# Expert activations turned by VectorE in 32x32 blocks, down weights read in whole rows, combine in a split one-pass format, final norm reordered

## The chip, the core and the metric

One core of one Trainium2 chip runs the whole program. The metric is the device time of one execution, in microseconds, as the median of several runs. All numbers are float32.

## What is computed

A decoder trunk of two layers on 256 tokens of 1024 features. Layer 0 (a state-space mixer, stick-breaking attention and a dense feed-forward block) and the attention of layer 1 are not touched by the change. What it touches is the routed feed-forward block of layer 1 and the last norm:

```python
def moe_swiglu(h, w_router, w_gate, w_up, w_down):
    logits = (h @ w_router).astype(F32)
    top_val, top_idx = lax.top_k(logits, TOP_K)
    gates = jax.nn.softmax(top_val, axis=-1)
    combine = jnp.sum(jax.nn.one_hot(top_idx, N_EXPERTS, dtype=F32) * gates[..., None], axis=-2)
    out = jnp.zeros_like(h)
    for e in range(N_EXPERTS):
        y_e = swiglu(h, w_gate[e], w_up[e], w_down[e])
        out = out + combine[..., e:e + 1].astype(h.dtype) * y_e
    return out
...
x = x + moe_swiglu(...)
return rmsnorm(x, final_norm)
```

There are 8 experts, 2 for each token. w_gate and w_up of an expert are 1024 x 3584, w_down is 3584 x 1024.

## The kernel before

The expert stage begins when the router has placed each token in a slot of each expert (at most 96 slots, in 3 groups of 32; a loop at the end of the program, `rest`, is for experts with more, and is skipped otherwise). The loop at L1485 goes over the experts. Each expert's hidden width of 3584 is worked in two halves h of 1792 (`HALF`), and a half lies in four quarters of 448 (`CW`) on four bands of 32 partitions: partition 32j + s holds slot s of a group, and quarter j of its columns. So one group's half is a tile of 128 x 448.

For each half, `side` (L1352) multiplies the gathered tokens `he` with the gate weights, in eight steps k over the 1024 inputs. A step takes one weight tile of 128 x 1792 from the ring, and for each group g and quarter j issues a matmul of 32 columns of weights (the tokens) against 448 moving columns; the four quarters use four column bands of the array. Each matmul in full float32 is two instructions in the trace. The result is in three PSUM banks `gu`, one for each group. `fn(..., AF.Silu)` on ScalarE writes `A`; a second `side` does the up weights; and VectorE multiplies bank and `A` back into `A` (L1514). The `gu` banks come in turn from a pool of four (`pg`).

The down projection contracts over the hidden width, so that width must be turned onto the partitions. `turn` (L1365) does so with TensorE transposes of 128 x 128 through a PSUM bank `mt` and a copy by ScalarE or VectorE into `aT`. For the first three of the seven 128-column blocks it is called after steps k = 2, 3 and 4 of the second half's gate; for the other four blocks after the third, fourth and fifth tile of the down stage. `down` (L1377) takes 14 weight tiles: `down_rows` (L227) reads, for a block i, 128 rows of two quarters j, each row 4 KB; the block that lies across both halves is two transfers of 64 partitions. The result is in two `yb` banks, and copied to `y`.

`back` (L1338) makes `selT`, the matrix of zeros and ones that puts slots back to tokens. `combine` (L1400) multiplies it with `y`, one token block t of 128 at a time, with four row bands of 32 partitions into four banks `cb`; VectorE adds each bank, times the router's weight, to `yacc`. The combine of expert e stands after steps k = 1 and 3 of the first gate half of expert e + 1; the last expert's stands in the final norm, from L1526.

The order of TensorE's instructions here is that of the program text (`InOrder`). The other engines' order is set by the framework's scheduler. Weight tiles go round a ring of 8 KB slots; `in_turn` (L217) issues their loads alternately from SyncE's and ScalarE's queue, when `give` reports a slot free, in the order in which they are used.

Of the kernel before, what the change touches and what calls it, by code (L numbers as in the profile page):

```python
# [18 lines left out]
P = 128  # L19
T = 256  # L20
D = 1024
KD = D // P
# [7 lines left out]
HALF = FFE // 2  # L30
CW = HALF // 4
NG = 3
CAP = 32 * NG
# [133 lines left out]
def trunk_kernel(  # L167
# [5 lines left out]
    nc = tc.nc  # L173
# [52 lines left out]

    def down_rows(e, i, j):  # L227

        v = [moe_w_down[0, e, h * HALF:(h + 1) * HALF, :].rearrange("(j c) f -> c j f", j=4)[:, j:j + 2]
             for h in range(2)]  # L230
        c0 = (i * P) % CW

        def load(t):
            t3 = t.rearrange("p (j f) -> p j f", j=2)
            if i == 3:
                in_turn(t3[0:64], v[0][CW - 64:CW])
                in_turn(t3[64:P], v[1][0:64])
            else:
                in_turn(t3, v[i // 4][c0:c0 + P])
        W.add(load, D, split=False)  # L240

# [17 lines left out]
    for r0 in range(0, D, 256):  # L259
        rows_of(od_w_out[0], r0)  # L260

    DOWN = [(i, j) for i3 in ((0, 1, 2), (3,), (4, 5, 6)) for i in i3 for j in (0, 2)]
    for e in range(NE):
        for h in range(2):
            for src in (moe_w_gate, moe_w_up):
                for k in range(KD):
                    half_row(src, e, k, h)
        for i, j in DOWN:
            down_rows(e, i, j)

# [906 lines left out]
    tri = me.tile([P, P], F32, name="tri", tag="y")  # L1177
    xg = me.tile([P, KD, T], F32, name="xg", tag="A")
    io8 = m0.tile([P, 2, NE], F32, name="io8")
# [158 lines left out]
    def back(e):  # L1338


        s4 = gq.tile([P, 2, NG * P], F32, name="sel4", tag="v1")
        selT[e] = me.tile([P, 2, NG, P], F32, name="selT", tag="selT")
        for t in range(2):
            vec.tensor_scalar(s4[:, t], io4.rearrange("p g j s -> p (g j s)"), pos[:, t, e:e + 1], None, op0=OP.is_equal)
        for t in range(2):
            b = bank("sT")
            for g in range(NG):
                seq.transpose(b[:, g * P:(g + 1) * P], s4[:, t, g * P:(g + 1) * P], ident)
            act.copy(selT[e][:, t].rearrange("p g s -> p (g s)"), b[:, :NG * P])
            yield  # L1350
# [13 lines left out]

    def turn(e, g, i0, i1):  # L1365

        b = bank("mt")
        n = (i1 - i0) * P
        for i in range(i0, i1):
            seq.transpose(b[:, (i - i0) * P:(i - i0 + 1) * P], A[e][:, g, i * P:(i + 1) * P], ident)  # L1370
        o = aT[e][:, g, i0:i1].rearrange("p i s -> p (i s)")
        if g % 2:
            vec.tensor_copy(o, b[:, :n])  # L1373
        else:
            act.copy(o, b[:, :n])  # L1375

    def down(e):  # L1377

        ys = [bank("yb", 1) for _ in range(2)]
        yd[e] = [ys[0][:, 0:256], ys[0][:, 256:512], ys[1][:, 0:256]]  # L1380
        for n, (i, j0) in enumerate(DOWN):
            s, w = W.take()
            w = w.rearrange("p (j f) -> p j f", j=2)
            for jj in range(2):
                j = j0 + jj
                for g in range(NG):
                    for q in range(4):
                        qs = slice(32 * q, 32 * q + 32)
                        seq.matmul(yd[e][g][qs], aT[e][:, g, i, 32 * j:32 * j + 32], w[:, jj, q * 256:(q + 1) * 256],
                                  start=n == 0 and jj == 0 and g % 2 == 0, stop=n == len(DOWN) - 1 and jj == 1,  # L1390
                                  skip_group_check=True)
            W.give(s)
            yield
        y = me.tile([P, NG, 256], F32, name="y", tag="y")
        act.copy(y[:, 0:2].rearrange("p g c -> p (g c)"), ys[0])
        vec.tensor_copy(y[:, 2], ys[1][:, 0:256])  # L1396
        yb[e] = y
        yield

    def combine(e, t):  # L1400

        bs = [bank("cb", 1), bank("cb"), bank("cb", 1), bank("cb")]
        for g in range(NG):
            for q in range(4):
                qs = slice(32 * q, 32 * q + 32)
                seq.matmul(bs[q][:, 0:256], selT[e][qs, t, g], yb[e][qs, g], start=g == 0, stop=g == NG - 1,
                          skip_group_check=True)
# [77 lines left out]
    for e in range(NE):  # L1485
        A[e] = me.tile([P, NG, 2 * CW], F32, name="A", tag="A")
        aT[e] = me.tile([P, NG, 7, P], F32, name="aT", tag="aT")
        for h in range(2):
            cs = slice(h * CW, (h + 1) * CW)
            gate = side(e)  # L1490
            bg = next(gate)
            for k in range(KD):
                run(gate, 1)
                if h == 0 and e and k in (1, 3):
                    combine(e - 1, k // 2)
                if h == 1 and k in (2, 3, 4):
                    turn(e, k - 2, 0, 3)
            for g in range(NG):
                fn(A[e][:, g, cs], bg[g][:, :CW], AF.Silu)
            up = side(e)  # L1500
# [12 lines left out]
            for g in range(NG):  # L1513
                vec.tensor_mul(A[e][:, g, cs], bu[g][:, :CW], A[e][:, g, cs])  # L1514
        dn = down(e)
        for n in range(len(DOWN)):
            run(dn, 1)
            if 1 < n < 5:
                turn(e, n - 2, 3, 7)
        if e == NE - 1:  # L1520
# [4 lines left out]
    e = NE - 1  # L1525
# [5 lines left out]
    for t in range(2):  # L1531
        combine(e, t)
        act.activation(sq, yacc[:, t], AF.Square, accum_out=s1[:, t:t + 1])
        pool_e.tensor_mul(yg[:, t], yacc[:, t], gf)  # L1534
        fn(s1[:, t:t + 1], s1[:, t:t + 1], AF.Sqrt, scale=1.0 / D, bias=epst)
        vec.reciprocal(s1[:, t:t + 1], s1[:, t:t + 1])
        for h in range(2):
            o = yg[:, t, h * 512:(h + 1) * 512]
            if h:
                act.activation(o, o, AF.Copy, scale=s1[:, t:t + 1])  # L1540
            else:
                vec.tensor_scalar(o, o, s1[:, t:t + 1], None, op0=OP.mult)
            (act if h else nc.sync).dma_start(out[0, t * P:(t + 1) * P, h * 512:(h + 1) * 512], o)

# [53 lines left out]
```

## Time and profile before

| | before |
|---|---|
| median of 3 runs | 1477.6 us (1477.43 to 1479.35) |
| profiled execution | 1477.57 us |
| span of its trace | 1475.5 us |
| mean granted TensorE clock | 0.991 |
| TensorE busy | 1438.1 us (97%) |
| VectorE, ScalarE, GpSimd busy | 394.8, 321.0, 134.9 us |
| read from HBM | 423.10 MB |

Busy time counts an engine's instructions; TensorE's weight loads are a row of their own (PEld), and lie beside its matmuls. The span is the profiled execution without what lies around it. The expert stage begins at about 500 us and takes some two thirds of the span. A granted clock of 1 is the higher of TensorE's two levels.

### The profile page before, as it was taken

What the parts mean: (1) busy time and instruction counts of PE and PEld (TensorE: products, weight loads), DVE (VectorE), ACT (ScalarE), POOL (GpSimd) and SP (SyncE); (2) the same over time, 40 slices, a digit from 0 to 9 for tenths busy, and PEclk for the clock granted to TensorE, in tenths of its full rate; (3) what the DMA queues carried; (4) which work ended last, traced back from release to release, by engine and by line L of the source; (5) the groups of instructions that cost most, each with busy time, mean ns of one, the idle gap of its engine ahead of it and who ended that gap; (6) DMA issues with size and microseconds to landing.
All of it is one profiled execution on the core that took longest, in us unless ns stands there. A gap on an engine that the chain in (4) does not pass through costs nothing.

```text
span 1475.5 us, 35199 instructions
## 1 busy us (share of the span) xinstructions
PE 1438.1 (97%) x16087; PEld 869.5 (59%) x16087; DVE 394.8 (27%) x696; ACT 321.0 (22%) x554; POOL 134.9 (9%) x223
## 2 busy tenths in 40 slices
PE   7899999999999999999999999999999999999995
PEld 6779999999788535534534543543453453354343
DVE  7666855558555200100010010010001001001001
ACT  5674643445544200000000000000000000000101
POOL 5960100002331000000000000000000000000001
PEclk9999999999999999999999999999999999999998
DMA  7324755555654699999999999999999999999950
GB/s 254 119 73 134 248 191 179 177 173 200 212 208 150 248 363 382 359 377 350 388 355 338 401 346 335 401 358 377 350 381 366 354 385 353 333 408 343 361 202 33
DMA packets 119774, 426.56 MB, mean 289 GB/s; under 512 B 14952, under 2 KB 41664, under 8 KB 119616
## 3 DMA queue, kind: packets, MB, share of 16 engines
q1 hardware_dynamic: 81376, 252.57, 47.8%
q10 hardware_dynamic: 38240, 171.64, 32.1%
q8 instruction: 130, 2.13, 0.6%
q14 instruction: 28, 0.23, 0.0%
HBM read 423.10 MB, written 1.06 MB: 287 GB/s over the span
## 4 chain that ended last, share of the span: by engine, by line
PE 91%; POOL 4%; DVE 2%; ACT 1%; issue 1%; DMA 0%; SPq 0%; POOLq 0%; DVEq 0%; ACTq 0%
PE gu L134 40%; PE yb L134 20%; PE fg L388 3%; PE fg L387 3%; PE fg L386 3%; PE oa L386 2%; PE oa L387 2%; PE ga L134 2%; PE oa L388 2%; PE mt L139 2%; PE cb L134 2%; PE pj L386 1%; PE pj L388 1%; PE pj L387 1%; POOL tmp L454 1%; POOL tmp L456 1%
## 5 line engine op out<-in xcount | busy, mean ns | idle before, releaser
L134 PE MATMUL gu<-w,he 128*32 128x448 f32 x6144 | 592.9, 540 | 0.3 <-ACT yacc L1208 0.3
L134 PEld LDWEIGHTS gu<-w,he 128*32 128x32 f32 x6144 | 193.9, 110 | 353.3 <-issue 345.5
L134 PE MATMUL yb<-w,aT 128*32 128x256 f32 x5376 | 296.5, 379 | 0.0
L134 PEld LDWEIGHTS yb<-w,aT 128*32 128x32 f32 x5376 | 172.3, 110 | 117.8 <-issue 6.8
L100 DVE TENSOR_TENSOR lo<-w,hi 128x1024 fp32r<-128x1024 f32 (+1 forms) x126 | 161.2, 1312 | 53.3 <-ACT hi L99 53.1
L99 ACT CAST hi<-w 128x1024 fp32r<-128x1024 f32 (+1 forms) x126 | 125.1, 1040 | 130.0 <-issue 85.2
L388 PE MATMUL fg<-glo,hi 128*128 128x256 f32 x352 | 99.9, 284 | 1.3 <-DVE glo L337 1.3
L386 PE MATMUL fg<-ghi,hi 128*128 128x256 f32 x352 | 99.6, 283 | 0.0
L387 PE MATMUL fg<-ghi,lo 128*128 128x256 f32 x352 | 99.4, 282 | 0.0
L1534 POOL TENSOR_TENSOR yg<-yacc,gf 128x1024 f32<-128x1024 f32 x2 | 4.7, 2350 | 979.2 <-DVE yacc L1410 979.2
L1375 ACT COPY aT<-mt 128x384 f32<-128x384 f32 (+1 forms) x32 | 17.1, 533 | 334.7 <-PE mt L139 305.1
L1514 DVE TENSOR_TENSOR A<-gu,A 128x448 f32<-128x448 f32 x48 | 30.0, 625 | 173.2 <-PE gu L134 164.4
L388 PEld LDWEIGHTS fg<-glo,hi 128*128 128x128 f32 x352 | 67.4, 191 | 2.1 <-DVE glo L337 2.1
L161 ACT ACTIVATE A<-gu 128x448 f32<-128x448 f32 x48 | 26.1, 544 | 193.5 <-PE gu L134 193.5
L386 PE MATMUL pj<-ghi,hi 128*128 128x256 f32 x224 | 65.4, 294 | 2.2 <-ACT hi L99 2.2
L386 PEld LDWEIGHTS fg<-ghi,hi 128*128 128x128 f32 x352 | 67.4, 191 | 0.0
L387 PEld LDWEIGHTS fg<-ghi,lo 128*128 128x128 f32 x352 | 67.4, 191 | 0.0
L387 PE MATMUL pj<-ghi,lo 128*128 128x256 f32 x224 | 64.5, 290 | 2.4 <-DVE lo L100 2.4
L388 PE MATMUL pj<-glo,hi 128*128 128x256 f32 x224 | 63.7, 287 | 1.0 <-DVE glo L623 1.0
L1396 DVE COPY y<-yb 128x256 f32<-128x256 f32 x8 | 3.4, 425 | 208.8 <-PE yb L134 208.8
L1373 DVE COPY aT<-mt 128x384 f32<-128x384 f32 (+1 forms) x16 | 10.0, 624 | 162.7 <-PE mt L139 162.7
L387 PE MATMUL oa<-hh,lo 128*128 128x256 f32 x176 | 49.5, 282 | 0.0
(351 smaller groups left out, 1510.3 us busy)
## 6 DMA issues: line engine op xcount, KB each, us to landing
w<-in_moe_w_gate_dram SPq DMA_DIRECT2D x69, 896.0 KB, 6.7
w<-in_moe_w_up_dram SPq DMA_DIRECT2D x68, 896.0 KB, 7.2
w<-in_moe_w_up_dram ACTq DMA_DIRECT2D x60, 896.0 KB, 7.0
w<-in_moe_w_gate_dram ACTq DMA_DIRECT2D x59, 896.0 KB, 8.1
w<-in_moe_w_down_dram ACTq DMA_DIRECT2D x48, 1024.0 KB, 8.6
w<-in_moe_w_down_dram SPq DMA_DIRECT2D x48, 1024.0 KB, 7.3
w<-in_od_w_in_dram SPq DMA_DIRECT2D x12, 1024.0 KB, 5.0
w<-in_ffn_w_gate_dram SPq DMA_DIRECT2D x11, 1024.0 KB, 7.1
```

Of the source, the lines that this page charges most:

```text
L99: ins = self.nc.scalar.copy(h[:, s], src[:, s]).ins
L100: ins2 = self.nc.vector.tensor_sub(l[:, s], src[:, s], h[:, s].bitcast(F32)).ins
L134: r = self.pe.matmul(*a, **k)
L139: r = self.pe.transpose(*a, **k)
L161: ins = self.act.activation(*a, **k).ins
L386: first = pe.matmul(o, whi, rhi, start=start, stop=False, skip_group_check=True).ins
L387: pe.matmul(o, wlo, rhi, start=False, stop=False, skip_group_check=True)
L388: return first, pe.matmul(o, whi, rlo, start=False, stop=stop, skip_group_check=True).ins
L454: eng.tensor_tensor(t[1], a_im, b_im, op=OP.mult)
L456: eng.tensor_tensor(t[3], a_im, b_re, op=OP.mult)
L1375: act.copy(o, b[:, :n])
L1514: vec.tensor_mul(A[e][:, g, cs], bu[g][:, :CW], A[e][:, g, cs])
```

## The change

The transposes on TensorE are gone. `turn` is called once for each group and half, right after the up matmuls: VectorE multiplies bank and `A` into a new tile `M`, with the 448 columns taken as 32 x 14 and written as 14 x 32, and one VectorE instruction transposes the 32 x 32 blocks of `M` into `aT`. By this a partition of `aT` holds 14 neighbouring hidden features, and `down_rows` reads for each partition two whole neighbouring rows, 8 KB in one piece; the partitions' pieces are 56 KB apart. `A` now holds one half. `y` is kept as a high part in the one-pass format (float32r), written by ScalarE, and a low part, the rest, written by VectorE; `selT` is float32r as well. `combine` runs the matmuls on both parts. In the final norm, VectorE makes the first 512 columns from `yacc` in one instruction with the reciprocal, GpSimd multiplies the other 512 only, and the last combine's second token block uses four banks of another pool.

```diff
+NB = CW // 32
-    def down_rows(e, i, j):
-        v = [moe_w_down[0, e, h * HALF:(h + 1) * HALF, :].rearrange("(j c) f -> c j f", j=4)[:, j:j + 2]
-             for h in range(2)]
...
-                in_turn(t3, v[i // 4][c0:c0 + P])
+    def down_rows(e, h, b):
+        v = moe_w_down[0, e, h * HALF:(h + 1) * HALF, :].rearrange("(p b) f -> p b f", b=NB)[:, b:b + 2]
+        W.add(lambda t: in_turn(t.rearrange("p (b f) -> p b f", b=2), v), D, split=False)
...
-        selT[e] = me.tile([P, 2, NG, P], F32, name="selT", tag="selT")
+        selT[e] = me.tile([P, 2, NG, P], F32R, name="selT", tag="selT")
...
-    def turn(e, g, i0, i1):
-        b = bank("mt")
-        n = (i1 - i0) * P
-        for i in range(i0, i1):
-            seq.transpose(b[:, (i - i0) * P:(i - i0 + 1) * P], A[e][:, g, i * P:(i + 1) * P], ident)
-        o = aT[e][:, g, i0:i1].rearrange("p i s -> p (i s)")
-        if g % 2:
-            vec.tensor_copy(o, b[:, :n])
-        else:
-            act.copy(o, b[:, :n])
+    def turn(e, g, h, bank_):
+        m = me.tile([P, CW], F32, name="M", tag="M")
+        vec.tensor_mul(m.rearrange("p (b c) -> p c b", c=32), bank_[:, :CW].rearrange("p (c b) -> p c b", b=NB),
+                       A[e][:, g].rearrange("p (c b) -> p c b", b=NB))
+        vec.transpose(aT[e][:, g, h], m)
...
-        y = me.tile([P, NG, 256], F32, name="y", tag="y")
-        act.copy(y[:, 0:2].rearrange("p g c -> p (g c)"), ys[0])
-        vec.tensor_copy(y[:, 2], ys[1][:, 0:256])
+        y = me.tile([P, 2, NG * 256], F32R, name="y", tag="y")
+        for i, b in enumerate(ys):
+            n = 512 - 256 * i
+            act.copy(y[:, 0, 512 * i:512 * i + n], b[:, :n])
+            vec.tensor_sub(y[:, 1, 512 * i:512 * i + n], b[:, :n], y[:, 0, 512 * i:512 * i + n].bitcast(F32))
...
-    def combine(e, t):
-        bs = [bank("cb", 1), bank("cb"), bank("cb", 1), bank("cb")]
+    def combine(e, t, kinds=(1, 0, 1, 0)):
+        bs = [bank("cb", k) for k in kinds]
         for g in range(NG):
-            for q in range(4):
-                qs = slice(32 * q, 32 * q + 32)
-                seq.matmul(bs[q][:, 0:256], selT[e][qs, t, g], yb[e][qs, g], start=g == 0, stop=g == NG - 1,
-                          skip_group_check=True)
+            for part in range(2):
+                for q in range(4):
+                    qs = slice(32 * q, 32 * q + 32)
+                    seq.matmul(bs[q][:, 0:256], selT[e][qs, t, g], yb[e][qs, part, g * 256:(g + 1) * 256],
+                               start=g == 0 and part == 0, stop=g == NG - 1 and part == 1, skip_group_check=True)
...
-                if h == 1 and k in (2, 3, 4):
-                    turn(e, k - 2, 0, 3)
...
-                vec.tensor_mul(A[e][:, g, cs], bu[g][:, :CW], A[e][:, g, cs])
+                turn(e, g, h, bu[g])
...
-            if 1 < n < 5:
-                turn(e, n - 2, 3, 7)
...
-        combine(e, t)
+        combine(e, t, (2, 2, 2, 2) if t else (1, 0, 1, 0))
         act.activation(sq, yacc[:, t], AF.Square, accum_out=s1[:, t:t + 1])
-        pool_e.tensor_mul(yg[:, t], yacc[:, t], gf)
+        pool_e.tensor_mul(yg[:, t, 512:], yacc[:, t, 512:], gf[:, 512:])
         fn(s1[:, t:t + 1], s1[:, t:t + 1], AF.Sqrt, scale=1.0 / D, bias=epst)
+    for t in range(2):
         vec.reciprocal(s1[:, t:t + 1], s1[:, t:t + 1])
...
+        vec.scalar_tensor_tensor(yg[:, t, :512], yacc[:, t, :512], s1[:, t:t + 1], gf[:, :512], op0=OP.mult, op1=OP.mult)
+        act.activation(yg[:, t, 512:], yg[:, t, 512:], AF.Copy, scale=s1[:, t:t + 1])
```

How the instructions stand, at three places. On TensorE, in the second half of the first expert, before (gu and ga are matmuls of the gate and up weights and of the gather, mt the transposes; w is a weight tile with its number):

```order
L134 MATMUL gu<-w_5398,he 32x448 x12
L134 MATMUL gu<-w_5442,he 32x448 x12
L139 MATMUL mt<-ident,A 128x128 x3
L134 MATMUL gu<-w_5456,he 32x448 x12
L139 MATMUL mt<-ident,A 128x128 x3
L134 MATMUL gu<-w_5470,he 32x448 x12
L139 MATMUL mt<-ident,A 128x128 x3
L134 MATMUL gu<-w_5484,he 32x448 x12
L134 MATMUL gu<-w_5498,he 32x448 x12
```

and now:

```order
L135 MATMUL gu<-w_5398,he 32x448 x12
L135 MATMUL gu<-w_5442,he 32x448 x12
L135 MATMUL gu<-w_5456,he 32x448 x12
L135 MATMUL gu<-w_5470,he 32x448 x12
L135 MATMUL gu<-w_5484,he 32x448 x12
L135 MATMUL gu<-w_5498,he 32x448 x12
```

The matmuls follow one another; the down stage loses its three visits of four transposes in the same way, and the combine's x12 becomes x24.

On VectorE, from the second up half of the first expert to its combine, before (seln picks the next expert's tokens, the rows with cb are the combine's updates):

```order
L1319 TENSOR_SCALAR seln<-iof,pos,rstdC 128x96 x2
L1514 TENSOR_TENSOR A<-gu,A 128x448 x3
L1373 COPY aT<-mt 128x512
L1396 COPY y<-yb 128x256
L1410 SCALAR_TENSOR_TENSOR yacc<-cb,gw,yacc 128x256 x8
```

and now:

```order
L1309 TENSOR_SCALAR seln<-iof,pos,rstdC 128x96 x2
L1358 TENSOR_TENSOR M<-gu,A 128x32x14
L1360 STREAM_TRANSPOSE aT<-M 128x448
L1358 TENSOR_TENSOR M<-gu,A 128x32x14
L1360 STREAM_TRANSPOSE aT<-M 128x448
L1358 TENSOR_TENSOR M<-gu,A 128x32x14
L1360 STREAM_TRANSPOSE aT<-M 128x448
L1383 TENSOR_TENSOR y<-yb,y 128x512
L1383 TENSOR_TENSOR y<-yb,y 128x256
L1398 SCALAR_TENSOR_TENSOR yacc<-cb,gw,yacc 128x256 x8
```

A transpose stands between two products, at the end of either half, and the copy of y has become two subtracts.

On VectorE at the end of the program, before (s holds the reciprocal roots of the final norm):

```order
L1396 COPY y<-yb 128x256
L1410 SCALAR_TENSOR_TENSOR yacc<-cb,gw,yacc 128x256 x4
L1536 RECIPROCAL s_12978<-s_12978 128x1
L1542 TENSOR_SCALAR yg<-yg,s_12978 128x512
L1410 SCALAR_TENSOR_TENSOR yacc<-cb,gw,yacc 128x256 x4
L1536 RECIPROCAL s_12978<-s_12978 128x1
L1542 TENSOR_SCALAR yg<-yg,s_12978 128x512
```

and now:

```order
L1383 TENSOR_TENSOR y<-yb,y 128x256
L1398 SCALAR_TENSOR_TENSOR yacc<-cb,gw,yacc 128x256 x4
L1519 RECIPROCAL s_12986<-s_12986 128x1
L1520 SCALAR_TENSOR_TENSOR yg<-yacc,s_12986,gf 128x512
L1398 SCALAR_TENSOR_TENSOR yacc<-cb,gw,yacc 128x256 x4
L1519 RECIPROCAL s_12986<-s_12986 128x1
L1520 SCALAR_TENSOR_TENSOR yg<-yacc,s_12986,gf 128x512
```

The second block's updates stand behind the first block's reciprocal and scaling in both; the scaling now reads `yacc` and the gains in place of GpSimd's product.

## Rows read from the trace of the kernel before

**Rows 1.** The page: span, busy time and share of each engine.
```profile
span 1475.5 us, 35199 instructions
...
PE 1438.1 (97%) x16087; PEld 869.5 (59%) x16087; DVE 394.8 (27%) x696; ACT 321.0 (22%) x554; POOL 134.9 (9%) x223
```
**Rows 2.** Waits of TensorE's weight loads, 560 to 1454 us: total, times, longest.
```profile
PEld gu L134 <- DVE A L1514: 3.4, 14, 0.2
PEld yb L134 <- DMA w<-in_moe_w_gate_dram: 1.2, 7, 0.2
```
**Rows 3.** The chain in order of time, one expert: start us, us, what.
```profile
864.20 1.51 PE cb L134 x24
...
887.24 13.67 PE gu L134 x144
900.90 0.48 PE mt L139 x3
...
907.12 13.67 PE gu L134 x144
...
936.25 7.77 PE yb L134 x144
...
951.23 23.45 PE yb L134 x432
...
985.34 1.51 PE cb L134 x24
986.85 15.92 PE gu L134 x168
```
**Rows 4.** Timeline, TensorE in layer 0, one-pass matmuls: start us, us of each.
```profile
300.00 0.28 PE L386 MATMUL oa<-hh,hi 128*128 128x256 f32 x1
300.12 0.28 PE L387 MATMUL oa<-hh,lo 128*128 128x256 f32 x1
```
**Rows 5.** Groups by form, VectorE, both stages: busy us, mean ns, idle before.
```profile
L1514 DVE TENSOR_TENSOR A<-gu,A 128x448 f32<-128x448 f32 x45 | 28.1, 625 | 168.2 <-PE gu L134 164.4
...
L545 DVE TENSOR_TENSOR Bex<-bcn,masks 128x512 f32<-128x512 f32 x8 | 8.7, 1094 | 2.1 <-POOL bcn L457 2.1
...
L402 DVE TENSOR_TENSOR hl<-us,hh 128x512 fp32r<-128x512 f32 x11 | 7.5, 685 | 0.2 <-ACT hh L402 0.2
...
L402 DVE TENSOR_TENSOR cx<-fav,cx 128x256 fp32r<-128x256 f32 x8 | 3.4, 420 | 7.7 <-ACT cx L402 7.7
```
**Rows 6.** Timeline, VectorE, end of a first up half: start, us, count, idle before.
```profile
1013.91 2.13 DVE L1514 TENSOR_TENSOR A<-gu,A 128x448 f32<-128x448 f32 x3 [4.75 <-PE gu L134]
```
**Rows 7.** Transfers: windows (last: clock, DMA share, GB/s), first down issue, first use, landings.
```profile
936.00:948.00 12.00, 12.00 (x208) 7.00 (x204) 0.93 (x3) 0.59 (x1) 0.00 (x0) 1.00 1.02 418
...
1013.09 9.39 ACTq L220 DMA_DIRECT2D w<-in_moe_w_down_dram  x3
...
1057.39 7.77 PE yb L134 x144
...
DMA to landing us min/median/max: 5.4/8.4/16.5
```
**Rows 8.** Timeline, ScalarE and VectorE after the last down matmul.
```profile
1454.73 0.59 ACT L1395 COPY y<-yb 128x512 f32<-128x512 f32 x1 [22.50 <-PE yb L134]
...
1456.97 1.66 DVE L1410 SCALAR_TENSOR_TENSOR yacc<-cb,gw,yacc 128x256 f32<-128x256 f32 x4 [1.42 <-PE cb L134]
...
1460.16 0.16 DVE L1536 RECIPROCAL s<-s 128x1 f32<-128x1 f32 x1 [1.54 <-ACT s L161]
1461.15 0.48 DVE L1542 TENSOR_SCALAR yg<-yg,s 128x512 f32<-128x512 f32 x1 [0.82 <-POOL yg L1534]
1461.55 1.65 DVE L1410 SCALAR_TENSOR_TENSOR yacc<-cb,gw,yacc 128x256 f32<-128x256 f32 x4
1464.74 0.16 DVE L1536 RECIPROCAL s<-s 128x1 f32<-128x1 f32 x1 [1.54 <-ACT s L161]
...
1465.72 0.72 ACT L1540 ACTIVATE yg<-yg,s 128x512 f32<-128x512 f32 x1 [1.01 <-POOL yg L1534]
```

More of the change, by code (lines that the diff above doesn't have):

```diff
@@ L225, in half_row @@
         W.add(lambda t: in_turn(t[:, :HALF], v), HALF, split=False)
-    def down_rows(e, i, j):
-        v = [moe_w_down[0, e, h * HALF:(h + 1) * HALF, :].rearrange("(j c) f -> c j f", j=4)[:, j:j + 2]
-             for h in range(2)]
[L231 to L237, printed above, removed]
-            else:
-                in_turn(t3, v[i // 4][c0:c0 + P])
-        W.add(load, D, split=False)
+    def down_rows(e, h, b):
+        v = moe_w_down[0, e, h * HALF:(h + 1) * HALF, :].rearrange("(p b) f -> p b f", b=NB)[:, b:b + 2]
+        W.add(lambda t: in_turn(t.rearrange("p (b f) -> p b f", b=2), v), D, split=False)
     for c0 in (0, 512, 1024, 1536):
@@ L260, in trunk_kernel @@
         rows_of(od_w_out[0], r0)
-    DOWN = [(i, j) for i3 in ((0, 1, 2), (3,), (4, 5, 6)) for i in i3 for j in (0, 2)]
     for e in range(NE):
@@ L267, in trunk_kernel @@
                     half_row(src, e, k, h)
-        for i, j in DOWN:
-            down_rows(e, i, j)
+        for h in range(2):
+            for b in range(0, NB, 2):
+                down_rows(e, h, b)
     ident = const.tile([P, P], F32, name="ident")
@@ L1177, in trunk_kernel @@
     tri = me.tile([P, P], F32, name="tri", tag="y")
-    xg = me.tile([P, KD, T], F32, name="xg", tag="A")
+    xg = me.tile([P, KD, T], F32, name="xg", tag="aT")
     io8 = m0.tile([P, 2, NE], F32, name="io8")
@@ L1380, in down @@
         yd[e] = [ys[0][:, 0:256], ys[0][:, 256:512], ys[1][:, 0:256]]
[L1381 to L1386, printed above, removed]
-                    for q in range(4):
-                        qs = slice(32 * q, 32 * q + 32)
-                        seq.matmul(yd[e][g][qs], aT[e][:, g, i, 32 * j:32 * j + 32], w[:, jj, q * 256:(q + 1) * 256],
-                                  start=n == 0 and jj == 0 and g % 2 == 0, stop=n == len(DOWN) - 1 and jj == 1,
-                                  skip_group_check=True)
-            W.give(s)
-            yield
@@ L1394, in down @@
-        y = me.tile([P, NG, 256], F32, name="y", tag="y")
-        act.copy(y[:, 0:2].rearrange("p g c -> p (g c)"), ys[0])
-        vec.tensor_copy(y[:, 2], ys[1][:, 0:256])
+        for h in range(2):
+            for b in range(0, NB, 2):
+                s, w = W.take()
+                w = w.rearrange("p (b f) -> p b f", b=2)
+                for bb in range(2):
+                    for g in range(NG):
+                        for q in range(4):
+                            qs = slice(32 * q, 32 * q + 32)
+                            seq.matmul(yd[e][g][qs], aT[e][:, g, h, 32 * (b + bb):32 * (b + bb) + 32],
+                                       w[:, bb, q * 256:(q + 1) * 256], start=h + b + bb == 0 and g % 2 == 0,
+                                       stop=h == 1 and b + bb == NB - 1, skip_group_check=True)
+                W.give(s)
+                yield
@@ L1403, in combine @@
         for g in range(NG):
-            for q in range(4):
-                qs = slice(32 * q, 32 * q + 32)
-                seq.matmul(bs[q][:, 0:256], selT[e][qs, t, g], yb[e][qs, g], start=g == 0, stop=g == NG - 1,
-                          skip_group_check=True)
+            for part in range(2):
+                for q in range(4):
+                    qs = slice(32 * q, 32 * q + 32)
+                    seq.matmul(bs[q][:, 0:256], selT[e][qs, t, g], yb[e][qs, part, g * 256:(g + 1) * 256],
+                               start=g == 0 and part == 0, stop=g == NG - 1 and part == 1, skip_group_check=True)
@@ L1485, in trunk_kernel @@
     for e in range(NE):
-        A[e] = me.tile([P, NG, 2 * CW], F32, name="A", tag="A")
-        aT[e] = me.tile([P, NG, 7, P], F32, name="aT", tag="aT")
+        aT[e] = me.tile([P, NG, 2, CW], F32, name="aT", tag="aT")
         for h in range(2):
-            cs = slice(h * CW, (h + 1) * CW)
+            A[e] = me.tile([P, NG, CW], F32, name="A", tag="A")
             gate = side(e)
@@ L1495, in trunk_kernel @@
                     combine(e - 1, k // 2)
-                if h == 1 and k in (2, 3, 4):
-                    turn(e, k - 2, 0, 3)
             for g in range(NG):
-                fn(A[e][:, g, cs], bg[g][:, :CW], AF.Silu)
+                fn(A[e][:, g], bg[g][:, :CW], AF.Silu)
             up = side(e)
@@ L1513, in trunk_kernel @@
             for g in range(NG):
-                vec.tensor_mul(A[e][:, g, cs], bu[g][:, :CW], A[e][:, g, cs])
+                turn(e, g, h, bu[g])
         dn = down(e)
-        for n in range(len(DOWN)):
-            run(dn, 1)
-            if 1 < n < 5:
-                turn(e, n - 2, 3, 7)
+        run(dn, NB)
         if e == NE - 1:
@@ L1531, in trunk_kernel @@
     for t in range(2):
-        combine(e, t)
+        combine(e, t, (2, 2, 2, 2) if t else (1, 0, 1, 0))
         act.activation(sq, yacc[:, t], AF.Square, accum_out=s1[:, t:t + 1])
-        pool_e.tensor_mul(yg[:, t], yacc[:, t], gf)
+        pool_e.tensor_mul(yg[:, t, 512:], yacc[:, t, 512:], gf[:, 512:])
         fn(s1[:, t:t + 1], s1[:, t:t + 1], AF.Sqrt, scale=1.0 / D, bias=epst)
+    for t in range(2):
         vec.reciprocal(s1[:, t:t + 1], s1[:, t:t + 1])
+        vec.scalar_tensor_tensor(yg[:, t, :512], yacc[:, t, :512], s1[:, t:t + 1], gf[:, :512], op0=OP.mult, op1=OP.mult)
+        act.activation(yg[:, t, 512:], yg[:, t, 512:], AF.Copy, scale=s1[:, t:t + 1])
         for h in range(2):
[L1538 to L1543, printed above, removed]
+            (act if h else nc.sync).dma_start(out[0, t * P:(t + 1) * P, h * 512:(h + 1) * 512],
+                                              yg[:, t, h * 512:(h + 1) * 512])
     most = nc.values_load(cmax[0:1, 0:1], min_val=0, max_val=T)
```

1 line of the change is left out of this document (removed).

## The prediction

> **What bounds the kernel now.** I read the page first: TensorE is busy for 97% of the span [rows 1]. A busy share alone does not make an engine the bound, so the next view is the table of waits, for TensorE's weight loads in the expert stage: they waited for a weight transfer 1.2 us in all, and for VectorE 3.4 us in 14 waits of at most 0.2 us [rows 2]. Nothing feeds TensorE late, so in this stage a microsecond of TensorE work taken away is a microsecond of time, until another supply becomes late. The chain of waits, in order of time, then prices each kind of work [rows 3]: one expert takes 121.14 us (from the first combine at 864.20 to the same place at 985.34), and the reader sees expert matmuls (gu, yb) interrupted by short visits: transposes (mt) and combines (cb). The last view is the end of the kernel, where TensorE is done and a short chain over the other engines remains [rows 8].
>
> **Term 1, the transposes of the activations leave TensorE.** Three visits of three in the second gate half and three of four in the down stage, for every expert. A visit costs more than the 0.48 us that its three transposes take, since the matmuls around it restart, so I take whole stretches. From 887.24 to 920.79 (907.12 + 13.67) stand 336 gu instructions and three visits: 33.55 us. A dense run costs (15.92 - 13.67) / (168 - 144) = 0.09375 us for one more instruction, so 336 of them without interruption take 15.92 + 168 x 0.09375 = 31.67. The visits cost 1.88 us. The down stage runs from 936.25 to 974.68 (951.23 + 23.45): 38.43 us for 672 yb instructions (144, 48, 48 and 432) and three visits; at 23.45 / 432 each, 672 take 36.48. These visits cost 1.95 us. Together 3.83 us per expert, **30.6 us** for eight; I allow 0.8 us either way for the trace's rounding.
>
> **Term 2, the combine.** Now a combine is 24 instructions in 1.51 us, 62.9 ns each: 12 matmuls in full float32, two instructions each. After it there are 12 matmuls in the one-pass format for the high part and 12 for the low part, so the count of instructions stays at 24 and only what one takes changes. This format with 32-row tiles does not occur in the trace. With the whole array, 256 columns of it start 0.12 us apart [rows 4]. Four tiles abreast would make that 30 ns, and 24 would take 0.72 us: a gain of 0.79. The other end is no gain: the weights are as wide and as many as now, so if loading sets the 62.9 ns, nothing changes (a loss is a rival below). I take a value near the first end, because the full-precision tiles also come near four abreast: the yb instruction has the same 256 columns and takes 54.3 ns, against 62.9 in the combine, a ratio of 1.16. 30 x 1.16 = 35 ns, 24 x 35 = 0.84 us, a gain of 0.67. Of 16 combines 14 stand between gu matmuls: **9.4 us**, with bounds 0 and 11.1.
>
> **Term 3, VectorE takes over the transposes: nothing, while its new work is covered.** For each group the product is now written with a step of 32 elements, and a block transpose follows. At the end of the first up half this matters: the next gate half takes PSUM banks in turn out of four, its second group needs the bank that the first product frees, its third group the bank of the second product. The products start 0.75 us apart now (2.13 us for three of 0.625) [rows 5, 6], as their groups finish: 1013.91, 1014.66, 1015.41. TensorE goes straight on to the next half, so the third group's first matmul comes at about 1016.8, two groups after the third bank is full. For the product I bound 0.625 (as now) to 0.96 (1094 ns per 512 columns, the dearest product of this kind in the trace, scaled to 448) and take 0.63. For the block transpose, which the trace does not have, the nearest rows are VectorE's subtracts, 0.42 us at 256 columns; I bound 0.42 to 1.25 (two passes over 448 at 0.625) and take 0.63, a one-pass price. Then the second product ends at 1013.91 + 3 x 0.63 = 1015.80, 1.0 us early. At the dear ends it ends at 1013.91 + 0.96 + 1.25 + 0.96 = 1017.08: a stall of 0.3 to 0.4 us, 3 us over eight experts. The Trainium skill (VectorE: DVE Perf Modes, The three transpose paths) gives 311 ns for 128 x 128 in bfloat16; 3.5 times that is an estimate of 1.09 us, by which the second product ends at 1016.26 and the sum is unchanged. After the second up half nothing waits: the seven down tiles of the first half need only the first half's blocks, and give 18 us of cover (336 yb instructions). The split of y (a cast on ScalarE, a subtract on VectorE, twice) takes under 2 us, and the combine comes after two gate tiles, 48 x 0.09375 = 4.5 us.
>
> **Term 4, the end.** Combine of the first token block: now the y copy starts at 1454.73 and the first yacc update at 1456.97. Then: cast 0.59, subtract 0.69, second subtract 0.42 [rows 5] and the last four matmuls of 0.035 bring it to 1456.57; that leaves 0.4 us for the hand-overs between the engines, so I leave the first update where it is. The first reciprocal ends at 1460.32 in either kernel. Now VectorE waits for GpSimd, scales until 1461.63 and ends the second block's updates at 1461.55 + 1.65 = 1463.20. After: one 512-column update (0.69), four updates (1.65): 1462.66. From there to the second reciprocal's end is as now, so that falls from 1464.90 to 1464.36; and where ScalarE's last pass then waited for GpSimd until 1465.72, it starts at once: GpSimd took 2.5 us from 1463.20 on, and with half the columns it is done at about 1463.9. ScalarE's pass (0.72) ends at 1465.1 and not at 1466.44: **1.3 us**, bounds -0.5 (the split of y late) and 2.
>
> **Term 5, the transfers.** Bytes stay the same: 44.04 MB per expert (32 tiles of 917,504 bytes and 14 of 1,048,576). At the new pace of 121.14 - 3.83 - 1.34 = 116.0 us that is 380 GB/s. In the busiest stretch the queues moved 418 GB/s for 12 us [rows 7], by which an expert's weights need 105 us. A down tile is issued at 1013.09 and first used at 1057.39: 44 us ahead, and a landing takes 16.5 us at worst, so some 28 us of lead lie in between. I cost the transfers at nothing; the cover is that lead. Reading 8 KB runs rather than 4 KB ones could only matter beyond it.
>
> **Sum.** 30.6 + 9.4 + 1.3 = 41.3 us from the profiled execution's 1477.57 (span 1475.5 and 2.1 around it; the median of the runs is 1477.6, the same): **1436 us**.
>
> **Rivals.**
> (a) The one-pass tiles don't run abreast. For it: nothing in the trace shows this format in row tiles. Against: float32 tiles of the same shape overlap. At 0.12 us one after another a combine takes 2.88 us, 1.37 more than now: +19.2 in the loop and some 2 at the end in place of -9.4. 1477.6 - 30.6 - 1.3 + 21.2 = 1467 us. Chance 0.08.
> (b) The stream of weights can't exceed its present mean of 364 GB/s (44.04 MB in 121.14 us). Then the last tile lands when it does now, and TensorE gains only the lead: 28 us and the end's 1.3, so 1448 us. For it: the transfer engines show no idle time (a DMA share of 1.02 in [rows 7]). Against: they do so while moving 418 GB/s for 12 us, so the share is no measure of what they can carry. The Trainium skill (DMA: Bandwidth & Descriptors, Specifications) puts the limit of HBM for one core at about 358 GB/s; by that rule this rival would win, and the measured stretch speaks against it. Chance 0.07.
> (c) The other side: the down weights, read as 8 KB from each of 128 places 56 KB apart, come slower than the two closed blocks of now. It decides from the point where one expert's stream takes longer than 121.14 + 28 / 8 = 124.6 us: gate and up take 29.36 MB / 418 = 70.2, so down may take 54.4, which is 270 GB/s. At half of 418 down takes 70.2 and an expert 140.4: 8 x (140.4 - 124.6) = 126 us slower, 1604 us. For it: no down tile is read so now. Against: rows of 7 KB in steps of 14 KB (gate and up) show no loss. Chance 0.03.
> (d) The combine gains nothing (loads set its pace): 1477.6 - 30.6 - 1.3 = 1446 us; inside the range below.
>
> **How the numbers follow.** Forecast 0.80 (with d), (a) 0.08, (b) 0.07, (c) 0.03, and 0.02 for a new wait that eats the gain. Low end: 31.4 + 11.1 + 2 less gives 1433, and 2 for rounding: 1431. High end: 29.8 saved, combine 0, end 0, the stall of 3: 1451; this takes in (b), and leaves out (a) and (c). A measurement of this kernel can tell about 0.2%, 3 us, from no change. Faster: 0.80 + 0.08 + 0.07 and a little; slower: (c) and half of the rest.
>
> **What would show it.** Right: no mt rows; gu in unbroken runs of 336 through the second half; an expert in 116 us; cb x24 near 0.85 us; the stream at 380 GB/s with TensorE still not waiting for transfers; the last ScalarE pass starting right after the reciprocal. Wrong: weight loads of TensorE waiting for VectorE in the third group (term 3), for w transfers (b, c), or a combine of 1.5 us and more (d, a).

## The result and the profile after

The changed kernel takes **1440.59 us** (median of 4 runs, 1439.96 to 1442.08), against 1478.47 us for the kernel before beside it (1477.43 to 1480.48): a ratio of 0.9744, 95% interval 0.9727 to 0.9761. The forecast was 1436.0 us in a range from 1431 to 1451. The profiled execution took 1439.96 us. The page of the kernel after, to be read against [rows 1]:

```profile
span 1438.3 us, 34753 instructions
...
PE 1396.6 (97%) x15919; PEld 849.7 (59%) x15919; DVE 436.0 (30%) x736; ACT 306.2 (21%) x530; POOL 132.1 (9%) x223
```

TensorE has 41.5 us less work, VectorE 41.2 us more, and the span is 37.2 us shorter. So nearly all the work taken from TensorE became time, and nearly all that VectorE got is covered. Where this happened is read from the chain of waits, kernel after, one expert (start us, us, what), against [rows 3]:

```profile
872.79 31.83 PE gu L135 x336
...
920.09 36.26 PE yb L135 x672
...
960.86 0.91 PE cb L135 x20
...
966.42 0.91 PE cb L135 x24
967.33 15.92 PE gu L135 x168
...
1076.92 0.91 PE cb L135 x22
```

The runs of 336 gu and of 672 yb instructions are now whole; between them stands no mt. The first takes 31.83 us where the same instructions with three visits took 33.55, the second 36.26 where it was 38.43. A combine takes 0.91 us and not 1.51 (a count under 24 here comes from records missing in the trace). From a combine to the same place in the next expert it is 1076.92 - 960.86 = 116.06 us, 5.08 less than the 121.14 of before: 1.72 + 2.17 from the transposes and 2 x 0.60 from the combines make 5.09.

Did anything become late in exchange? First TensorE's weight loads in the expert stage, kernel after: what they waited for, us in total, times, longest. All rows that name another engine are shown; rows that name a transfer, as in [rows 2], are no longer there:

```profile
PEld gu L135 <- DVE M L1358: 5.1, 7, 0.7
...
PEld gu L135 <- PE yb L135: 1.7, 7, 0.2
PEld cb L135 <- DVE y L1383: 1.5, 1, 1.5
```

The wait for the product M comes once per expert, in the second gate half, at the bank that the second product frees, as term 3 of the prediction had it: in the next expert that product ends at 997.13 and the weight load that waited for it starts at 997.18. The last row is the last combine, which waits for y at the end. The weight transfers, kernel after: the window of one expert (last columns clock, DMA share, GB/s), and the landings of the tiles that are used in that stretch:

```profile
960.86:1076.92 116.06, 116.06 (x1530) 51.97 (x1530) 15.31 (x26) 6.05 (x12) 0.00 (x0) 1.00 1.00 381
```

```profile
DMA to landing us min/median/max: 5.3/7.2/11.2
```

The stream moves 381 GB/s on the mean of a whole expert, and a tile lands in at most 11.2 us where [rows 7] had 16.5. VectorE's groups by form, kernel after, for the two new operations (busy us, mean ns of one, idle before):

```profile
L1358 DVE TENSOR_TENSOR M<-gu,A 128x448 f32<-128x448 f32 x48 | 45.8, 955 | 188.8 <-PE gu L135 101.4 <-issue 83.1
L1360 DVE STREAM_TRANSPOSE aT<-M 128x448 f32<-128x448 f32 x48 | 31.0, 645 | 1.7
```

The product takes 955 ns, where the one without the step took 625 [rows 5]; the block transpose takes 645 ns. And the end, where the forecast said 1.3 us less: the timeline of the kernel after, ScalarE and VectorE, against [rows 8].

```profile
1416.07 0.86 ACT L1382 CAST y<-yb 128x512 fp32r<-128x512 f32 x2 [52.02 <-PE yb L135]
1416.69 1.02 DVE L1383 TENSOR_TENSOR y<-yb,y 128x512 fp32r<-128x512 f32 x2 [32.75 <-ACT y L1382]
...
1418.68 1.66 DVE L1398 SCALAR_TENSOR_TENSOR yacc<-cb,gw,yacc 128x256 f32<-128x256 f32 x4 [0.96 <-PE cb L135]
...
1422.15 0.75 DVE L1520 SCALAR_TENSOR_TENSOR yg<-yacc,s,gf 128x512 f32<-128x512 f32 x1
1422.82 1.65 DVE L1398 SCALAR_TENSOR_TENSOR yacc<-cb,gw,yacc 128x256 f32<-128x256 f32 x4
...
1426.27 0.72 ACT L1521 ACTIVATE yg<-yg,s 128x512 f32<-128x512 f32 x1 [0.29 <-DVE s L1519]
```

ScalarE's last pass starts right behind the reciprocal, as forecast, and GpSimd is no longer waited for. It ends 10.92 us after the cast of y began (1426.99 - 1416.07); before, it was 11.71 (1466.44 - 1454.73). The computation gains 0.8 us. But from there to the end of the span it is 11.3 us, and 9.1 before. From y to the end of the span: 22.2 us against 20.8.

So the 37.2 us of the span are: 39.5 us in the loop (from the first gu matmul to y, 493.20 to 1454.73 before and 494.02 to 1416.07 after: 961.53 and 922.05), less 1.4 at the end, less 0.8 because the expert stage began 0.8 us later in this execution; that start lies between 491.9 and 497.3 us in the runs below, and the change doesn't touch what precedes it.

### The profile page after: what moved, and what is told of

Same layout as the page of the kernel before. It is cut to its first block, busy times and chain, and to the rows that moved or that the text cites. A ratio compares the mean times of both kernels' runs of the same rounds, so it can differ in the third digit from the quotient of the medians.

```text
span 1438.3 us, 34753 instructions
## 1 busy us (share of the span) xinstructions
PE 1396.6 (97%) x15919; PEld 849.7 (59%) x15919; DVE 436.0 (30%) x736; ACT 306.2 (21%) x530; POOL 132.1 (9%) x223
## 4 chain that ended last, share of the span: by engine, by line
PE 90%; POOL 4%; DVE 2%; ACT 1%; issue 1%; DMA 0%; SPq 0%; DVEq 0%; ACTq 0%
PE gu L135 41%; PE yb L135 20%; PE fg L378 3%; PE fg L377 3%; PE fg L376 3%; PE oa L376 2%; PE oa L377 2%; PE ga L135 2%; PE oa L378 2%; PE pj L376 1%; PE pj L378 1%; PE pj L377 1%; PE cb L135 1%; POOL tmp L446 1%; POOL tmp L444 1%
## 5 line engine op out<-in xcount | busy, mean ns | idle before, releaser
L135 PE MATMUL yb<-w,aT 128*32 128x256 f32 x5376 | 291.5, 379 | 0.0
L1358 DVE TENSOR_TENSOR M<-gu,A 128x448 f32<-128x448 f32 x48 | 45.8, 955 | 188.8 <-PE gu L135 101.4
L1383 DVE TENSOR_TENSOR y<-yb,y 128x512 fp32r<-128x512 f32 (+1 forms) x16 | 8.2, 552 | 262.0 <-ACT y L1382 262.0
L1382 ACT CAST y<-yb 128x512 fp32r<-128x512 f32 (+1 forms) x16 | 6.9, 482 | 348.0 <-PE yb L135 348.0
L1334 DVE TENSOR_SCALAR sel<-io,pos 128x384 f32<-128x384 f32 x16 | 6.0, 417 | 150.0 <-PE sT L140 150.0
L1309 DVE TENSOR_SCALAR seln<-iof,pos,rstdC 128x96 f32<-128x96 f32 x16 | 4.6, 327 | 153.7 <-PE ga L135 153.6
## 6 DMA issues: line engine op xcount, KB each, us to landing
w<-in_moe_w_down_dram SPq DMA_DIRECT2D x56, 1024.0 KB, 10.1
```

Of the source, the lines that this page charges most:

```text
L135: r = self.pe.matmul(*a, **k)
L1358: vec.tensor_mul(m.rearrange("p (b c) -> p c b", c=32), bank_[:, :CW].rearrange("p (c b) -> p c b", b=NB), A[e][:, g].rearrange("p (c b) - ...
L1382: act.copy(y[:, 0, 512 * i:512 * i + n], b[:, :n])
L1383: vec.tensor_sub(y[:, 1, 512 * i:512 * i + n], b[:, :n], y[:, 0, 512 * i:512 * i + n].bitcast(F32))
```

## Experiments

**The theory** to be tested: the gain is TensorE time, 3.9 us per expert from the transposes and 0.6 for each combine; the whole rows and the new norm give nothing by themselves. **Rivals**: the longer runs of the down weights feed TensorE better; the stepped product costs time that the sum hides; the one-pass tiles run one after another with something else making up for it; the end got worse through its writes, or through what the program does after them. Each ratio is against the kernel before on the same chip, with its 95% interval.

**1. The turn and the rows, with the old combine and the old norm.** On the kernel after:

```diff
-        selT[e] = me.tile([P, 2, NG, P], F32R, name="selT", tag="selT")
+        selT[e] = me.tile([P, 2, NG, P], F32, name="selT", tag="selT")
...
+        act.copy(y[:, 0:2].rearrange("p g c -> p (g c)"), ys[0])
+        vec.tensor_copy(y[:, 2], ys[1][:, 0:256])
...
+                seq.matmul(bs[q][:, 0:256], selT[e][qs, t, g], yb[e][qs, g], start=g == 0, stop=g == NG - 1,
```

> The turn on VectorE with whole-row loads alone; combine, y and final norm as before. My theory (time comes from TensorE's visits): an expert in about 117.2 us (121.14 - 3.9), no mt rows, cb x24 still 1.51 us, time 1478.5 - 31 = about 1447 us. Rival (the combine and the norm carry a good part of the gain): 1455 us or more. Rival (whole rows, not TensorE's visits, give the gain): the same 1447 here, told apart by the run with whole rows alone.

Measured: 1447.51 us, ratio 0.9774 (0.9756 to 0.9791). The chain of this kernel, in order of time:

```profile
877.11 31.84 PE gu L135 x336
...
924.41 36.26 PE yb L135 x672
...
965.18 1.51 PE cb L135 x24
```

The gu and yb runs are those of the kernel after to 0.01 us, the combine is that of before. From the first gu matmul to y it is 930.14 us (494.84 to 1424.98): 31.4 of the 39.5 us in the loop belong to this part.

**2. The whole rows alone.** On the kernel before, the same bytes are read with the new addresses:

```diff
+        n = DOWN.index((i, j))
+        h, b = n // 7, 2 * (n % 7)
+        r = moe_w_down[0, e, h * HALF:(h + 1) * HALF, :].rearrange("(p b) f -> p b f", b=14)[:, b:b + 2]
...
-                in_turn(t3, v[i // 4][c0:c0 + P])
+                in_turn(t3, r)
```

> The kernel before with the down weights read in whole rows and nothing else; the hidden features and the weight rows don't match in this run, so its down products are of other pairs than the reference's. My theory: no change, within 2 us of 1478.5, since TensorE never waits for a transfer; the packets get longer (8 KB, some 0.31 us each). Rival (loads set part of the pace): faster by 5 us or more. Rival (rows 56 KB apart load slower): landings of down tiles rise beyond 17 us and the time with them.

Measured: 1480.8 us, ratio 1.0003 (0.9991 to 1.0016). Its chain, the same combine of two experts:

```profile
864.03 1.51 PE cb L134 x24
...
985.17 1.51 PE cb L134 x24
```

121.14 us per expert, to the hundredth that of before [rows 3]. The landings of the weight tiles:

```profile
DMA to landing us min/median/max: 5.8/7.3/9.5
```

The latest landing is 9.5 us against 16.5, and TensorE has no wait for a transfer left, but there was 1.2 us of it in the whole stage to win [rows 2]. This is no sign that whole rows come sooner: the 16.5 us of before belong to the block that was read in two transfers of 512 KB. Loads of the down weights, kernel before, 600 to 1400 us (KB each, median us to landing):

```profile
w<-in_moe_w_down_dram ACTq DMA_DIRECT2D x40, 1024.0 KB, 8.6
w<-in_moe_w_down_dram SPq DMA_DIRECT2D x40, 1024.0 KB, 7.4
...
w<-in_moe_w_down_dram SPq DMA_DIRECT2D x14, 512.0 KB, 13.7
```

In this kernel all are single transfers of 1024 KB, with medians of 9.4 and 9.0 us in the same stretch. The layout is needed for the block transpose, and gives nothing itself; rival (c) of the prediction falls, since the time doesn't move.

**3. The new norm alone**, on the kernel before (the diff of the final norm in the change, nothing else).

> The kernel before with the reordered final norm alone. My theory: the last ScalarE pass ends 1.0 to 1.4 us earlier after the last down matmul. Of the late landing of the output writes (5.1 us after the change, 2.3 before) two theories: it comes with the reorder (the two queues issue within 0.03 us of each other): landing 5 us again and the time about 1 to 2 us longer than before; it is where the fetch of the code that follows falls: landing anything between 2 and 5.5, not tied to the reorder.

Measured: 1479.7 us, ratio 1.0001 (0.9988 to 1.0015): nothing, with bounds of about 2 us either way. Its timeline, the two ends of the final stage on ScalarE:

```profile
1454.44 0.59 ACT L1395 COPY y<-yb 128x512 f32<-128x512 f32 x1 [22.50 <-PE yb L134]
...
1464.27 0.72 ACT L1539 ACTIVATE yg<-yg,s 128x512 f32<-128x512 f32 x1 [0.29 <-DVE s L1537]
```

The last pass ends 10.55 us after y began, 1.16 sooner than before: the forecast's 1.3 is there, in the computation. It does not reach the time. What changed with it is when the output writes land (from issue, us), in this kernel:

```profile
DMA to landing us min/median/max: 4.3/4.4/4.4
```

Before it was 2.1 to 2.5 us.

**4. The change without its norm**, on the kernel after: the old order of the final norm and the old banks.

> The changed kernel with the old final norm. My theory of the loop: as after the change, an expert in 116.06 us. Of the landing of the output writes: if it comes with the reorder, 2.3 us again, and the time 1439 to 1440; if it is where the code fetch falls, anything between 2 and 5.5, and with 5 the time is 1442.

Measured: 1440.56 us, ratio 0.9744 (0.9721 to 0.9767), the same as the whole change. The reorder is worth nothing in either company. The writes' landings in this kernel:

```profile
DMA to landing us min/median/max: 2.0/2.3/2.6
```

So late landing goes with the new norm. Beside experiment 1 this kernel shows the combine: from the first gu matmul to y 922.05 us (494.52 to 1416.57), 8.1 less than 930.14. The combine alone on the kernel before was not run.

**5. All output writes from one queue**, on the kernel after:

```diff
-            (act if h else nc.sync).dma_start(out[0, t * P:(t + 1) * P, h * 512:(h + 1) * 512],
+            nc.sync.dma_start(out[0, t * P:(t + 1) * P, h * 512:(h + 1) * 512],
```

> The changed kernel with all four output writes issued by SyncE (after the change two go out on each of two queues, 0.03 us apart). Theory one (two writes that start together on two queues hold each other up): the writes go out 0.35 us apart, landing 2.3 us again. Theory two (a code fetch at the moment when the writes start holds up one transfer engine): landing stays at 4 to 5 us, as the fetch stays where it is. The time: within 2 us of 1440.6 in either case.

Measured: 1438.94 us, ratio 0.9734 (0.9711 to 0.9756), and its writes:

```profile
DMA to landing us min/median/max: 4.8/4.9/5.0
```

They land as late from one queue, so it doesn't take two queues. The two writes of a block are under way together in this kernel too.

**6. The product without the step**, on the kernel after:

```diff
-        vec.tensor_mul(m.rearrange("p (b c) -> p c b", c=32), bank_[:, :CW].rearrange("p (c b) -> p c b", b=NB),
-                       A[e][:, g].rearrange("p (c b) -> p c b", b=NB))
+        vec.tensor_mul(m, bank_[:, :CW], A[e][:, g])
```

> The changed kernel with the product written and read in plain order, so that its hidden features don't meet their own down rows. My theory: the product falls from 956 to about 625 ns (the step of 32 elements is the cause), the runs of 336 gu instructions lose at most 0.1 us each, and the time stays within 1 us of 1440.6, since the cover was enough. Rival (VectorE's product is on the path, as TensorE's waits of 0.7 us on it say): 5 us faster.

Measured: 1438.25 us, ratio 0.9733 (0.9709 to 0.9758). VectorE's group in the expert stage, this kernel:

```profile
L1358 DVE TENSOR_TENSOR M<-gu,A 128x448 f32<-128x448 f32 x45 | 28.1, 625 | 186.4 <-PE gu L135 104.1 <-issue 78.3
```

The waits of the weight loads:

```profile
PEld gu L135 <- DVE aT L1359: 1.7, 7, 0.2
PEld gu L135 <- DVE M L1358: 1.7, 7, 0.2
```

And the chain, the run that begins with the second gate half:

```profile
870.29 31.71 PE gu L135 x336
```

The step costs 330 ns in each of 48 products, 16 us of VectorE. Of that TensorE feels 31.83 - 31.71 = 0.12 us per expert, 1 us in all, although the weight loads' waits for VectorE fall from 5.1 to 3.4 us: loads run ahead of the matmuls, and the rest of the wait is covered. The 1 us is inside the interval of the ratio; the chain shows it, and so does the stretch from the first gu matmul to y, 921.0 us (491.88 to 1412.90) where the kernel after has 922.05.

**7. Only the high part in the combine**, on the kernel after: half of its matmuls.

```diff
-            for part in range(2):
+            for part in range(1):
```

> The changed kernel with the combine on the high part of y alone: 12 matmuls for each combine and not 24, the low part is left out of the sum. If what a combine costs is its instructions at 0.03 to 0.037 us each, it falls from 0.91 to 0.50 us and an expert from 116.06 to 115.2, the time by 6 to 7 us. If it is mostly the switch to and from row tiles, by less than 3 us.

Measured: 1432.28 us, ratio 0.9681 (0.9661 to 0.9701). A combine in its chain:

```profile
957.72 0.56 PE cb L135 x9
...
1078.28 0.56 PE cb L135 x12
```

Twelve matmuls less take 0.91 - 0.56 = 0.35 us less, 0.029 us each. A quarter of the 0.12 us between one-pass matmuls on the whole array [rows 4] is 0.030: four tiles run abreast. What is left, 0.56 - 0.35 = 0.21 us, doesn't come from the number of matmuls, if the line through these two counts holds; no run has fewer than twelve. From the first gu matmul to y it is 917.0 us (492.98 to 1410.02), 5.0 less than in the kernel after, as 14 x 0.35 says.

**8. The second block's updates ahead of the first reciprocal**, on the kernel after, by a scheduling order alone:

```diff
-        vec.reciprocal(s1[:, t:t + 1], s1[:, t:t + 1])
+        issue_behind(tc, vec.reciprocal(s1[:, t:t + 1], s1[:, t:t + 1]).ins, added)
```

(`added` is the last of the second block's updates.)

> The changed kernel with the second token block's updates put ahead of the first block's reciprocal on VectorE, where they no longer wait for ScalarE's root. Expected from the rows of the changed kernel: the last ScalarE pass ends 1.5 to 2 us earlier (at 10.9 us after the end of the down stage now, at 9 then). If the program's end follows the output writes, the time falls by as much; if the end hangs on something else (code of the branches behind), less.

Measured: 1440.07 us, ratio 0.9729 (0.9711 to 0.9747). The last pass on ScalarE, in a timeline in which y began at 1419.44:

```profile
1427.56 0.72 ACT L1522 ACTIVATE yg<-yg,s 128x512 f32<-128x512 f32 x1 [0.30 <-DVE s L1520]
```

It ends 8.84 us after y, 2.1 sooner than in the kernel after, and the time doesn't move. Whatever ends this program is neither the last pass nor, by experiments 3 and 4, the landing.

**9. The three branches at the end of the program in one**, on the kernel after. They are for experts with more than 96 tokens and are never taken here:

```diff
-    for first, n in ((CAP, CAP), (CAP + P, P)):
-        with tc.If(most > first):
-            vec.tensor_scalar(pos, pos, -float(n), None, op0=OP.add)
-            with tc.For_i(0, NE, 1) as e:
-                rest(e)
     with tc.If(most > CAP):
+        again(CAP)
+        with tc.If(most > CAP + P):
+            again(P)
```

(`again` holds the lines taken out.)

> The changed kernel with the three branches at the program's end (for experts with more tokens than slots, never taken here) nested in one. Theory: after the output writes the program still goes through three branches, each with a fetch of code that lies 2.1 to 2.8 us behind the one before; one branch saves two of these steps, 4 us: 1436 to 1437 us. Rival (the end follows the landing of the output writes): no change, within 1.5 us of 1440.6.

Measured: 1436.01 us, ratio 0.9724 (0.9702 to 0.9746). SyncE's queue waits for itself at these branches. In the kernel after:

```profile
SPq L1529 <- SPq L1529: 8.0, 3, 4.4
```

in this one:

```profile
SPq L1533 <- SPq L1533: 5.9, 2, 3.8
```

and in the kernel before, which has three branches:

```profile
SPq L1548 <- SPq L1548: 5.9, 2, 3.6
```

So this row doesn't tell the price of a branch, and neither do the medians, since the intervals of this kernel and of the change overlap. What tells it is the end by itself. From the first gu matmul to y this kernel takes the same as the kernel after (922.07 us, 491.92 to 1413.99, and 922.05); the stage began 2.1 us sooner in this execution, and the edit touches nothing ahead of it; from y to the end it is 19.1 us against 22.2.

**10. Experiments 8 and 9 together.**

> The same with the second token block's updates ahead of the first block's reciprocal as well. Theory of the branches: the last ScalarE pass ends 2 us earlier than in the changed kernel, and with one branch this is not given back: 1434 to 1436 us. Rival: as the run with the moved updates alone, 1440.

Measured: **1433.98 us**, ratio 0.9703 (0.9685 to 0.972), below the interval of the change itself: the version that beats both kernels. Of the 6.6 us between its median and that of the change 5.0 lie behind y in the profiled executions (17.2 and 22.2). Its last pass, with y at 1415.00:

```profile
1423.12 0.72 ACT L1522 ACTIVATE yg<-yg,s 128x512 f32<-128x512 f32 x1 [0.30 <-DVE s L1520]
```

The ends of all these kernels side by side, in us, from the timelines, the writes' landings and the spans:

| | branches | y to last pass | write lands after | last pass to end | y to end |
|---|---|---|---|---|---|
| before | 3 | 11.7 | 2.3 | 9.1 | 20.8 |
| 2, rows alone | 3 | 11.7 | 2.3 | 10.8 | 22.5 |
| 1, turn and rows | 3 | 11.7 | 2.3 | 10.1 | 21.8 |
| 4, old norm | 3 | 12.1 | 2.3 | 10.1 | 22.2 |
| 3, new norm alone | 3 | 10.6 | 4.4 | 10.2 | 20.8 |
| the change | 3 | 10.9 | 5.1 | 11.3 | 22.2 |
| 5, one queue | 3 | 10.9 | 4.9 | 10.1 | 21.0 |
| 6, dense product | 3 | 10.9 | 5.0 | 10.9 | 21.8 |
| 7, high part alone | 3 | 8.5 | 4.8 | 12.6 | 21.1 |
| 8, updates first | 3 | 8.8 | 4.8 | 12.7 | 21.6 |
| 9, nested | 1 | 10.9 | 3.8 | 8.2 | 19.1 |
| 10, both | 1 | 8.8 | 3.5 | 8.4 | 17.2 |

With three branches y to the end is 20.8 to 22.5 us, whether the last pass comes 8.5 or 12.1 us after y; the second and the first row end in the same code and differ by 1.7. With one branch the last column follows the second: 2.1 us less computation, 1.9 us less to the end. This rests on one pair of executions; the medians (1436.01 and 1433.98) fit, but their intervals overlap. So at the end of the program the branches are what is waited for, as long as there are three of them. The transfers in the packed traces fit this. When the writes are done, pieces of 8 KB from an instruction queue still follow one another, 0.9 to 2.8 us apart: three in each of the ten kernels with three branches (in the kernel after at 1432.43, 1434.59 and 1436.69, with the end at 1438.3), two in each with one branch (in experiment 9 at 1429.97 and 1432.06, with the end at 1433.1).

## Why the prediction held, and where not

**The bound: right.** TensorE is at 97% before and after, and 41.5 us less work gave 37.2 us less span.

**Term 1 (30.6): right.** The prediction's 1.88 and 1.95 us per expert came as 1.72 and 2.17, 31.1 for eight; experiment 1 shows 31.4 in the loop. The layout gives none of it (experiment 2).

**Term 2 (9.4, bounds 0 and 11.1): right in kind, 1 us too high.** Measured 0.60 us for a combine and not 0.67: 14 x 0.60 = 8.4, and 8.1 between experiments 1 and 4. The tiles do run four abreast, at 0.030 rather than the 0.035 taken; what was missed are some 0.2 us per combine that don't come from the number of its matmuls (experiment 7). Rival (a), tiles that don't run abreast, and (d), no gain at all, both fall by it.

**Term 3 (0): right to 1 us, with the product's price off.** The product stands at the dear bound, 955 ns, and not at 0.63 us; the transpose is 0.645 us, as taken. The dear product delays the second gate half by 0.12 us per expert (experiment 6), a third of the stall at the dear ends, and this lies already in the 31.83 above; without it the run takes 31.71, against 31.67 worked out, so the transpose adds next to nothing. The estimate of 1.09 us from the Trainium skill (VectorE: DVE Perf Modes, The three transpose paths) is well above the measured 0.645, which decides.

**Term 4 (1.3, bounds -0.5 and 2): the term that was mis-sized.** Its step was to put down the earlier end of ScalarE's last pass as earlier end of the kernel. Two things went wrong in it. The pass came 0.8 us sooner and not 1.3: the first yacc update stands 2.61 us behind the start of y (1418.68 - 1416.07), not the unchanged 2.24 of [rows 8], so the split of y costs 0.4 us here; and the 512-column update takes 0.75, not 0.69. And none of the 0.8 arrived: what follows the last pass got longer by as much and more (9.1 to 11.3 us), since the end hangs on the branches after it. The profile of before gave a sign that the prediction did not read: 9.1 us between the last pass and the end of the span. The measured +1.4 is itself no size of the change, since ends with the same code differ by 1.7; experiments 3 and 4 put the norm at nothing.

**Term 5 (0): right.** 381 GB/s against 380 forecast, and no wait for a transfer. Rival (b), a stream held at 364 GB/s, falls: had it held, TensorE would have waited for w. The Trainium skill's figure (DMA: Bandwidth & Descriptors, Specifications), about 358 GB/s of HBM for one core, is a stack's 716 GB/s divided by two cores; the prediction took it as a limit that would decide here. Here one core runs, and it moves 381 GB/s over a whole expert.

**The sum.** 41.3 was forecast and 37.2 came in the span: 2.7 of the difference is term 4, 0.8 the start of the expert stage in this execution, and some 0.5 the loop.

**What stays open.** Why the writes land at 4.3 to 5.2 us with the new norm and at 2.0 to 2.6 with the old one, as long as there are three branches. It is not the number of queues (experiment 5), and it does not set the time (experiments 3 and 4). The transfers in the packed traces give a hint. Of the 288 packets of the first block's writes 255 have started after 1.5 us in the kernel after (1423.75 to 1425.25), and the other 33 take until 1427.5; with the old norm (experiment 4) all have started within 1.7 us (1424.72 to 1426.36). In the kernel after two transfers of 16 KB of instructions run meanwhile (1423.24 to 1425.88); with the old norm the two of that size come between the writes of the two blocks (1426.36 to 1428.78). A collision of the two fits. But in experiment 9 only pieces of 8 KB run beside the second block's writes, and these still land after some 3.8 us; a run that separates the two was not made.

## What to carry to other kernels

Where one engine has no waits left, price a visit from whole stretches of the chain (33.55 us with visits, 31.67 without), not by its own instructions: that sum came out within 0.5 us in 31. What the work costs on the engine that takes it over mattered little here, with that engine busy for 30%: 16 us more of VectorE for the step cost TensorE 1 us, at the one buffer that VectorE holds back, and this buffer is what to look for. Before a saving near the end is counted, look at what lies between the last computation and the end of the span: 0.8 to 2.9 us of earlier computation were worth nothing there, until two branches that are never taken were put inside a third.

## What the runs showed of the hardware that was not expected

- Writing 448 float32 columns with a step of 32 elements took VectorE's product (one operand in PSUM) from 625 to 955 ns; a transpose of 32 x 32 blocks over 128 x 448 float32 took 645 ns, no more than a dense product.
- One-pass matmuls of 256 columns on 32-row tiles took 0.91 us for 24 and 0.56 us for 12: 0.029 us each, four abreast, and some 0.2 us for a group of them between other matmuls.
- With three branches that aren't taken at its end the span ended 22.2 us after y, with one 19.1, and with one and the reordered updates 17.2; with three the reordered updates alone gave 21.6.
- The same 256 KB writes landed after 2.3 or after 5.1 us, by the order of the work ahead of them, with no effect on the time (1440.56 and 1440.59 us).
